# Dilated heads with the values as weights and turned outputs, and the mixture of dilations on GpSimd from SyncE's loads

## Chip, cores, metric

One core of a Trainium2 chip runs the kernel. The metric is device time in microseconds, the median of the runs. The core's engines work beside each other, each on its own queue in order: TensorE (matrix products; in the profile PE, and PEld for its weight loads), VectorE (DVE), ScalarE (ACT), GpSimd (POOL) and SyncE (SP, which here only issues DMAs; GpSimd issues some too). A matrix instruction holds one operand in the array, the weights, and streams the other through it; its result lands in PSUM, from where VectorE or ScalarE takes it to SBUF. A product of fp32 operands is two such instructions.

## What is computed

An encoder layer over two sequences, of 1024 and 256 rows (1280 in all, ten tiles of 128). Two attention branches run in parallel on the same input: eight windowed heads with a sink, and twelve dilated heads, four for each of the dilations 1, 4 and 16. Each dilated head attends within its residue class; the three dilations of one head are then mixed with a softmax over their log-sums:

```
def _dilated_mixture(q, k, v, bias_b):
    for gi, (window, dil) in enumerate(B_GROUPS):            # (128,1), (512,4), (2048,16)
        hs = slice(gi * 4, (gi + 1) * 4)
        o, lse = _banded_attention(_to_residues(q[:, :, hs], dil), _to_residues(k[:, :, hs], dil),
                                   _to_residues(v[:, :, hs], dil), window // (2 * dil), dil, bias_b[:, hs], None)
        outs.append(_from_residues(o, dil)); lses.append(_from_residues(lse, dil))
    alpha = jax.nn.softmax(jnp.stack(lses), axis=0)
    return jnp.sum(alpha[..., None] * jnp.stack(outs), axis=0)

merged = gate0 * (o_a @ w_branch_a) + gate1 * (o_b @ w_branch_b)
x = x + merged @ w_out
```

Gates, output product, a squared-ReLU MLP and two norms follow. The large products are carried out in three passes over operands split into a rounded high part and a low rest.

## The kernel before

The queue order of every engine is written out by hand, as generators whose steps are drawn at fixed places; nothing is reordered. Four stages matter here.

*Values and pairs.* The input product is made column block by column block (`pair`, products `seven`, `prompt` and `six`, L351). `tick` is called between parts of it; in the last seven of sixteen pairs every second tick draws one step of `attention_b`.

*Dilated heads*, `attention_b`. `order` has 60 tiles: two head pairs, three dilations, ten tiles of 128 queries in residue order. A tile is one piece of 128 queries against 256 or 128 keys or, at the two ends of a sequence or residue class, two pieces of 64 queries, each with its own 128 keys. A step handles two tiles. In this order it issues: the value loads; `values_of` and `store_values` for the tiles of two steps before; `transposes` for those of the step before (L553); `scores` (products L522, bias and maximum L533); `exponentials` with their sums (L543). `values_of` (L566) holds the turned probabilities `pt` (128 keys x 128 queries) as weights and streams 64 columns of v for each head, so its output has queries on the partitions and the two heads side by side. `store_values` takes one tile on ScalarE and one on VectorE into `o`, a row of 2*64 outputs, two negated maxima and two sums (`ROW`, 132 numbers), and GpSimd stores it to `scr_b` (L575), 72 stores in all.

*Windowed heads*, the loop at L1275: 40 tiles, two per iteration j, with `scores`, `exponential`, `transposes` and `values_of` (L1110) like those above, only that `values_of` here holds 64 columns of v as weights and streams 128 columns of `pt`, each head's output in its own half of the partitions. The output tile `o` (two buffers) is stored by GpSimd (L1114). Between them the loop draws from `fill`, the gate products `logits` (L192): a weight column block is fetched by SyncE (`fetch`, L222), split by ScalarE and VectorE (`prepare`, L231, L235), and results go to `scr_g` through SyncE (L1136). GpSimd loads the next unit's bias (L454).

The same loop draws twice per iteration, from j = 4 on, from `merges`: for each head pair and each two tiles `load_rows` has GpSimd load the rows of the three dilations back in natural order (L1148 to L1159, 76 loads in all), and `merge` makes on VectorE the mixture weights from the maxima and sums (L1167 to L1178), weighs the rows (L1182) and adds them (L1187, L1188) into `merged`, 128 queries to a partition block. At the loop's end, and in the next stage at places listed in `side`, `turn_merged` turns a tile with two TensorE transposes (L1216) and ScalarE makes its high part `ob_hi` (L1224); `low_b` makes the low part (L1228). The next stage is the list `jobs`, gated branch products (L192 again), which read `ob_hi` and `ob_lo` as the streamed operand.

Tiles come from tags with a fixed number of buffers: `wslot` ("w", ten of 4 KB a partition, for weights, gate results and the rows `r`), `slot` ("m", 33), PSUM banks by tag ("mm" 3, "sc" 2, "pt" 2, "pv" 1). An instruction that writes a tile waits until the buffer's earlier readers are done.

## Time and profile before

| | |
|---|---|
| time before, median of 3 runs | 1723.88 us (1721.58 to 1724.01) |
| the profiled execution | 1723.0 us, its span 1721.2 us |
| granted TensorE clock | 0.999 |
| stage of the dilated heads | about 356 to 535 us |
| stage of the windowed heads and the mixture | about 555 to 710 us |
| branch products (`jobs`) from | about 712 us |

The span runs from the first to the last instruction. A row of the order of time gives start, length, engine, line of the kernel, operation, output and inputs, shapes and how many were put together; in square brackets stands idle time before it and what ended it. For a matrix instruction `pv<-v,pt 128*128 128x64` is: into pv, weights of 128 rows by 128 columns, a streamed operand of 128 partitions by 64 columns. Its printed length contains the run through the array, which overlaps the next one's; the distance from start to start is what it costs. A row of a group gives, after the count, busy time in us, the mean ns of one, and idle time before it with what ended it.

### The profile page before, as it was taken

Reading aid. Unit: us, or ns where it says so; the run is one execution under the profiler, and the core shown is the slowest. Engines: PE = TensorE matmul, PEld = TensorE weight load, DVE = VectorE, ACT = ScalarE, POOL = GpSimd, SP = SyncE. Lnnn points to the kernel's source line nnn. Section 1 sums busy time; section 2 is a strip of 40 time slices with the busy share of each in tenths; the row PEclk is TensorE's granted clock in tenths of the full one; section 3 lists DMA queues with packets and bytes.
Section 4 is the critical chain, followed back from the end, with each engine's and each line's share of the span. In section 5 each row is a group of like instructions: output and inputs, shape, how many; then the busy total and the mean of one; then the engine's idle time right before and its main releaser. Section 6 shows DMA issues by size and latency. Waiting matters only on the chain.

```text
span 1721.2 us, 25157 instructions
## 1 busy us (share of the span) xinstructions
PE 1690.8 (98%) x9248; PEld 1430.4 (83%) x9248; DVE 973.6 (57%) x1688; ACT 727.0 (42%) x1528; POOL 516.2 (30%) x442
## 2 busy tenths in 40 slices
PE   7999999999999999999999999999999999999998
PEld 6898888888888888788888788888888888888886
DVE  6732323445553566677368545455556876667575
ACT  6232323355553555655166333333334433333344
POOL 0213222212322244300100445565555342314140
PEclk9999999999999999999999999999999999999999
DMA  6414343576666753656012334433446834633333
GB/s 239 145 43 140 115 137 95 150 196 178 173 171 176 208 174 104 221 181 230 25 74 74 122 120 157 149 115 127 157 136 232 308 130 158 209 115 117 117 116 123
DMA packets 213738, 256.34 MB, mean 149 GB/s; under 512 B 24487, under 2 KB 144123, under 8 KB 213488
## 3 DMA queue, kind: packets, MB, share of 16 engines
q1 hardware_dynamic: 200704, 228.26, 41.1%
q0 software_dynamic: 11824, 24.38, 4.6%
q10 hardware_dynamic: 1088, 2.10, 0.3%
q8 instruction: 73, 1.20, 0.3%
q14 instruction: 49, 0.40, 0.1%
HBM read 169.10 MB, written 90.73 MB: 151 GB/s over the span
## 4 chain that ended last, share of the span: by engine, by line
PE 87%; DVE 4%; ACT 2%; issue 2%; DMA 2%; POOL 1%; SPq 0%; DVEq 0%; ACTq 0%; POOLq 0%
PE dn L351 21%; PE x L351 18%; PE mm L192 12%; PE z L351 9%; PE v L739 5%; PE pv L351 5%; PE mm L351 5%; PE y L351 4%; PE pv L566 2%; PE sc L522 2%; PE pt L553 1%; PE pv L1110 1%; PE pt L1095 1%; PE tr L342 1%; DVE clo L318 1%
## 5 line engine op out<-in xcount | busy, mean ns | idle before, releaser
L351 PE MATMUL dn<-dhi,ulo 128*128 128x512 f32 x448 | 174.6, 390 | 2.9 <-DVE ulo L186 2.9
L351 PE MATMUL dn<-dlo,uhi 128*128 128x512 f32 x448 | 174.3, 389 | 0.0
L351 PE MATMUL dn<-dhi,uhi 128*128 128x512 f32 x448 | 174.3, 389 | 0.0
L351 PE MATMUL x<-chi,wlo 128*128 128x512 f32 x424 | 167.6, 395 | 2.0 <-DVE u L1760 1.4
L351 PE MATMUL x<-clo,whi 128*128 128x512 f32 x424 | 165.7, 391 | 0.1
L351 PE MATMUL x<-chi,whi 128*128 128x512 f32 x424 | 165.1, 389 | 0.0
L318 DVE TENSOR_TENSOR wlo<-ta,whi 128x1024 fp32r<-128x1024 f32 x30 | 55.7, 1857 | 180.9 <-ACT whi L316 180.9
L318 DVE TENSOR_TENSOR wlo<-raw,whi 128x1024 fp32r<-128x1024 f32 x60 | 89.4, 1491 | 102.2 <-ACT whi L316 102.2
L393 POOL TENSOR_TENSOR tb<-raw 128x512 f32<-128x512 f32 x25 | 33.6, 1345 | 340.8 <-PE mm L192 114.9
L351 PEld LDWEIGHTS dn<-dhi,ulo 128*128 128x128 f32 x448 | 84.1, 188 | 21.4 <-DVE ulo L186 3.9
L186 DVE TENSOR_TENSOR ulo<-uraw,uhi 128x1024 fp32r<-128x1024 f32 x56 | 95.2, 1720 | 11.7 <-ACT uhi L185 11.7
L351 PEld LDWEIGHTS dn<-dhi,uhi 128*128 128x128 f32 x448 | 84.1, 188 | 17.5
L351 PEld LDWEIGHTS dn<-dlo,uhi 128*128 128x128 f32 x448 | 84.1, 188 | 17.3
L351 PEld LDWEIGHTS x<-chi,wlo 128*128 128x128 f32 x424 | 79.7, 188 | 20.3 <-issue 3.1
L351 PEld LDWEIGHTS x<-chi,whi 128*128 128x128 f32 x424 | 79.6, 188 | 17.2
L351 PEld LDWEIGHTS x<-clo,whi 128*128 128x128 f32 x424 | 79.8, 188 | 14.8 <-DVE clo L318 0.4
L1585 POOL TENSOR_TENSOR t<-raw,t 128x1024 f32<-128x1024 f32 x16 | 46.0, 2897 | 143.1 <-DMA raw<-in_w_down_dram 143.1
L1736 DVE TENSOR_TENSOR v<-v,dn 128x512 f32<-128x512 f32 x90 | 59.5, 682 | 42.8 <-PE dn L351 38.7
L1832 POOL TENSOR_TENSOR u<-u,u 128x640 f32<-128x640 f32 x16 | 25.6, 1598 | 162.4 <-ACT u L1757 162.4
L351 PE MATMUL pv<-phi,wlo 128*128 128x256 f32 x256 | 72.5, 283 | 1.7 <-ACT u L1756 1.7
L351 PE MATMUL dn<-dhi,up 128*128 128x512 f32 x224 | 73.5, 389 | 0.0
L543 ACT ACTIVATE s<-s,o 128x128 f32<-128x128 f32 (+1 forms) x120 | 51.9, 434 | 50.5 <-DVE o L535 46.5
(338 smaller groups left out, 4724.2 us busy)
## 6 DMA issues: line engine op xcount, KB each, us to landing
scr_u<-u SPq DMA_DIRECT2D x112, 320.0 KB, 2.6
uraw<-scr_u SPq DMA_DIRECT2D x56, 512.0 KB, 4.2
raw<-in_w_in_dram SPq DMA_DIRECT2D x33, 512.0 KB, 6.0
raw<-in_w_up_dram SPq DMA_DIRECT2D x32, 512.0 KB, 5.4
raw<-in_w_down_dram SPq DMA_DIRECT2D x28, 512.0 KB, 6.5
sg<-scr_g SPq DMA_DIRECT2D x32, 256.0 KB, 6.2
uraw<-scr_u SPq DMA_DIRECT2D x28, 256.0 KB, 4.7
v<-scr_v SPq DMA_DIRECT2D x96, 64.0 KB, 2.4
```

What stands on the lines that cost most here:

```text
L186: nc.vector.tensor_tensor(lo, src, hi.bitcast(F32), op=ALU.subtract)
L192: nc.tensor.matmul(ps, a, b, start=i == 0, stop=i == len(seq) - 1)
L318: nc.vector.tensor_tensor(lo, src, hi.bitcast(F32), op=ALU.subtract)
L351: nc.tensor.matmul(ps, a, b, start=first and i == 0, stop=last and i == len(seq) - 1, skip_group_check=True)
L393: (nc.vector if vector else nc.gpsimd).tensor_tensor(o, x, y, op=ALU.subtract)
L522: nc.tensor.matmul(at(k, h)[p0 : p0 + nq, :], qk[rows, p0 : p0 + nq], qk[rows, P + P * a : P + P * a + W], start=True, stop=True, skip_gro ...
L543: nc.scalar.activation(s[:, h, :W], s[:, h, :W], AF.Exp, bias=nm[:, h : h + 1], accum_out=l[:, h : h + 1])
L566: nc.tensor.matmul(pv[p0 : p0 + nq, HD * h : HD * h + HD], pt[:, 2 * k + h, p0 : p0 + nq], v[:, a + k, HALVES[h]], start=k == 0, stop=k == ...
L739: nc.tensor.matmul(ps[:, :n], a, b, start=k == 0 and j == 0, stop=k == KC - 1 and j == 2)
L1585: nc.gpsimd.tensor_tensor(o, a, b, op=ALU.subtract)
L1736: nc.vector.tensor_tensor(v, v, ps, op=ALU.add)
L1832: nc.gpsimd.tensor_tensor(u[S1], u21, u22, op=ALU.add)
```

## The change

Dilated heads. `values_of` now holds 64 columns of v as weights and streams `pt`, the heads alternating innermost, into the two halves of the partitions: outputs have head and channel on the partitions and queries along the row. `store_values` takes both tiles of a step with one copy, on VectorE and ScalarE in turn, and stores runs of queries that are contiguous into `scr_b[g][i]` (128 x 1280), 54 stores in all. Maxima and sums no longer go with the rows; they stay in two const tiles `nm_b`, `l_b` (128 x 120), at columns that `places` gives.

The mixture. `merge` is one generator. Once, it turns the two tiles of statistics (two TensorE transposes), copies them with VectorE, stores them with 13 GpSimd DMAs into `scr_n`, and reads them back with 12 (`spread`: each partition gets 1/32 of every class, in pieces of 16 to 128 bytes, 4,608 in all). After four more draws VectorE puts them into natural order and computes, for all heads at once, what the old `merge` computed for two tiles; the weights go back in residue order with 6 GpSimd DMAs to `scr_c`. Then 18 items follow, one per draw: block of up to 512 queries, head pair, dilation. SyncE loads the outputs and, for each head, its weights broadcast over 64 partitions (three DMAs an item, two items ahead); GpSimd multiplies and, for dilations 4 and 16, adds, reading across the residue classes, into `merged`, which is now turned as the products need it. `turn_merged` is gone; `high_b` and `low_b` split a whole block at once.

```
-    scr_b = [dram.tile([T, 2, ROW], F32, name=f"scr_b{g}_") for g in range(3)]
+    scr_b = [[dram.tile([P, T], F32, name=f"scr_b{g}{i}") for i in range(2)] for g in range(3)]
+    scr_n = dram.tile([2, ROWS * P], F32, name="scr_n")
+    scr_c = dram.tile([1, ROWS * P], F32, name="scr_c")
...
-                o = make("o", (P, ROW), n=8)
...
-                nc.vector.tensor_scalar(o[:, 2 * HD : 2 * HD + 2], m, -1.0, None, op0=ALU.mult)
-                live[k] = s, o
+                nc.vector.tensor_scalar(nm_b[:, places(k)], m, -1.0, None, op0=ALU.mult)
+                live[k] = s
...
-        def values_of(j, whole):
+            live[j] = pt
+
+        def values_of(j, pv):
 
             _, _, _, (pieces, W, _) = order[j]
-            pt, v = live[j][0], held.pop(j)[1]
-            pv = whole[:, P * (j % 2) : P * (j % 2) + P]
-            for h in range(2):
-                for a, (p0, nq, _, _) in enumerate(pieces):
-                    for k in range(W // P):
-                        nc.tensor.matmul(pv[p0 : p0 + nq, HD * h : HD * h + HD], pt[:, 2 * k + h, p0 : p0 + nq],
-                                         v[:, a + k, HALVES[h]], start=k == 0, stop=k == W // P - 1,
+            pt, v = live.pop(j), held.pop(j)[1]
+            c = P * (j % 2)
+            for a, (p0, nq, _, _) in enumerate(pieces):
+                for k in range(W // P):
+                    for h in range(2):
+                        nc.tensor.matmul(pv[HALVES[h], c + p0 : c + p0 + nq], v[:, a + k, HALVES[h]],
+                                         pt[:, 2 * k + h, p0 : p0 + nq], start=k == 0, stop=k == W // P - 1,
                                          skip_group_check=True)
 
-        def store_values(j, eng, whole):
-            g, i, _, (pieces, _, _) = order[j]
-            o = live.pop(j)[1]
-            moved(eng, o[:, : 2 * HD], whole[:, P * (j % 2) : P * (j % 2) + P])
-            for p0, nq, qa, _ in pieces:
-                nc.gpsimd.dma_start(scr_b[g][qa : qa + nq, i, :], o[p0 : p0 + nq, :])
+        def store_values(j, eng, pv):
+            o = make("o", (P, 2 * P), n=3)
+            moved(eng, o, pv[:, : 2 * P])
+            runs = []
+            for k in (j, j + 1):
+                g, i, _, (pieces, _, _) = order[k]
+                for p0, nq, qa, _ in pieces:
+                    c = P * (k % 2) + p0
+                    if runs and runs[-1][0] + runs[-1][2] == c and runs[-1][1] + runs[-1][2] == qa:
+                        runs[-1][2] += nq
+                    else:
+                        runs.append([c, qa, nq])
+            for c, qa, nq in runs:
+                nc.gpsimd.dma_start(scr_b[g][i][:, qa : qa + nq], o[:, c : c + nq])
...
-                store_values(j - 4, nc.scalar, pv)
-                store_values(j - 3, nc.vector, pv)
+                store_values(j - 4, (nc.vector, nc.scalar)[j // 2 % 2], pv)
...
-        def load_rows(i, t):
...
-        def merge(i, t):
-
-            r = rows_b.pop((i, t))
-            nm, ls = r[:, :, :, 2 * HD : 2 * HD + 2], r[:, :, :, 2 * HD + 2 :]
...
-                nc.vector.tensor_tensor(o, o, e[:, j].unsqueeze(3).to_broadcast([P, 3, 2, HD]), op=ALU.mult)
-            yield
-            if t // 4 not in merged:
-                merged[t // 4] = slot("merged", (P, 4, 2 * P))
-            m = merged[t // 4][:, t % 4 : t % 4 + 2, P * i : P * i + P]
-            nc.vector.tensor_tensor(m, r[:, :, 0, : 2 * HD], r[:, :, 1, : 2 * HD], op=ALU.add)
-            nc.vector.tensor_tensor(m, m, r[:, :, 2, : 2 * HD], op=ALU.add)
-            yield
-
...
+        def merge():
+
+            cb = slot("cb")
+            ps = bank("mm", "tn")
+            for i, x in enumerate((nm_b, l_b)):
+                nc.tensor.transpose(ps[:ROWS, P * i : P * i + P], x, ident)
+            rows = cb[:ROWS, : 2 * P].rearrange("p (x q) -> p x q", x=2)
+            nc.vector.tensor_copy(rows, ps[:ROWS, : 2 * P].rearrange("p (x q) -> p x q", x=2))
+            a = scr_n[:, :]
+
+            def dump(r0, n, step, c0, m, base, stride):
+                dst = bass.AP(a.tensor, a.offset + base, [[stride, n], [ROWS * P, 2], [1, m]])
+                nc.gpsimd.dma_start(dst, rows[r0 : r0 + (n - 1) * step + 1 : step, :, c0 : c0 + m])
+
+            for x in range(4):
+                dump(8 * x, 7, 1, 0, P, NS * x + 64, P)
...
+            dump(72, 48, 1, 0, P, 9 * NS, P)
...
+            for g in range(3):
+                for b, sl in ((0, slice(0, 32)), (2, slice(32, 40))):
+                    R = place(g, b)[3]
+                    for x in range(2):
+                        dst = (raw[:, g, x, sl] if g else nat[:, x, 0, sl]).rearrange("p (r j) -> p r j", r=R)
+                        nc.gpsimd.dma_start(dst, spread(scr_n, g, b, x))
...
+            for _ in range(5):
+                yield
+            for g in (1, 2):
+                for b, sl in ((0, slice(0, 32)), (2, slice(32, 40))):
+                    R = place(g, b)[3]
+                    nc.vector.tensor_copy(nat[:, :, g, sl].rearrange("p x (j r) -> p x j r", r=R),
+                                          raw[:, g, :, sl].rearrange("p x (r j) -> p x j r", r=R))
...
+                    nc.gpsimd.dma_start(spread(scr_c, g, b), out[:, g, sl].rearrange("p (r j) -> p r j", r=R))
+            yield
+            yield
...
+            items = [(b, i, g) for b in range(3) for i in range(2) for g in range(3)]
+            held = {}
+
+            def load(k):
+                if k >= len(items):
+                    return
+                b, i, g = items[k]
+                t0, n = BLOCKS[b]
+                base, length, stride, R = place(g, b)
+                r = held[k] = wslot("r", (P, 2, n))
+                q0, nq = t0 % NS // R, n // R
+                src = scr_b[g][i][:, NS:] if b == 2 else scr_b[g][i][:, :NS]
+                src = src.rearrange("p (r q) -> p r q", r=R)[:, :, q0 : q0 + nq]
+                nc.sync.dma_start(r[:, 0, :].rearrange("p (r q) -> p r q", r=R), src)
+                a = scr_c[:, :]
+                for h in range(2):
+                    nc.sync.dma_start(
+                        r[HALVES[h], 1, :].rearrange("p (r q) -> p r q", r=R),
+                        bass.AP(a.tensor, a.offset + base + (2 * i + h) * length + q0, [[0, HD], [stride, R], [1, nq]]))
+
+            load(0)
+            yield
+            load(1)
+            yield
+            for k, (b, i, g) in enumerate(items):
+                load(k + 2)
+                r = held.pop(k)
+                n = BLOCKS[b][1]
+                R = place(g, b)[3]
+                if b not in merged:
+                    merged[b] = slot("merged", (P, 2, n))
+                m = merged[b][:, i, :]
+                nc.gpsimd.tensor_tensor(r[:, 0, :] if g else m, r[:, 0, :], r[:, 1, :], op=ALU.mult)
+                if g:
+                    m = m.rearrange("p (q r) -> p q r", r=R)
+                    nc.gpsimd.tensor_tensor(m, m, r[:, 0, :].rearrange("p (r q) -> p q r", r=R), op=ALU.add)
+                yield
...
-        def turn_merged(t, tag="pt"):
...
-            for j in range(2):
-                nc.tensor.transpose(ps[:, P * j : P * j + P], merged[t // 4][:, t % 4, P * j : P * j + P], ident)
...
+        def high_b(b):
+
+            ob_hi.block(b)
+            ob_lo.block(b)
+            nc.scalar.activation(ob_hi.t[b, 0], merged[b], AF.Copy)
+
+        def low_b(b):
+            nc.vector.tensor_tensor(ob_lo.t[b, 0], merged[b], ob_hi.t[b, 0].bitcast(F32), op=ALU.subtract)
...
-        merges = merges_of([(i, t) for t in range(0, NT, 2) for i in range(2)])
+        merges = merge()
...
-                if j >= n - 4:
-                    turn_merged(j - n + 4, "mm")
...
-            if j >= n - 4 and j < n:
-                low_b(j - n + 4)
-                turn_merged(j - n + 5, "mm")
-                low_b(j - n + 5)
+            if j == n - 4:
+                high_b(0)
...
-        side = {0: [(turn_a, 0)], 1: [(low_a, 0), (turn_a, 1)], 2: [(low_a, 1), (turn_merged, 4)],
-                3: [(low_b, 4), (turn_a, 2), (widen, 4)], 4: [(low_a, 2), (turn_a, 3)], 5: [(low_a, 3), (turn_merged, 5)],
-                6: [(low_b, 5), (turn_merged, 6)], 7: [(low_b, 6), (turn_merged, 7)], 8: [(low_b, 7)],
+        side = {0: [(turn_a, 0)], 1: [(low_a, 0), (turn_a, 1)], 2: [(low_a, 1)],
+                3: [(turn_a, 2), (widen, 4)], 4: [(low_a, 2), (turn_a, 3)], 5: [(low_a, 3)],
+                6: [(high_b, 1)], 7: [(low_b, 1)],
                 9: [(turn_a, 4), (widen, 6)], 10: [(low_a, 4), (turn_a, 5)], 11: [(low_a, 5)],
                 13: [(turn_a, 6), (widen, 8)], 14: [(low_a, 6)], 15: [(turn_a, 7)], 16: [(low_a, 7)],
-                17: [(turn_merged, 8)], 18: [(low_b, 8), (turn_merged, 9)], 19: [(low_b, 9)],
+                17: [(high_b, 2)], 18: [(low_b, 2)],
                 20: [(turn_a, 8)], 21: [(low_a, 8)], 22: [(turn_a, 9)], 23: [(low_a, 9)]}
```

`place(g, b)` and `spread` only compute addresses: base, class length, stride and number of classes of dilation g in block b (1 class for dilation 1; 4 and 8 in the longer sequence, 2 and 2 in the shorter). In the branch stage `run(merges)` stands behind `sums_a()` instead of ahead of it.

113 lines of the change are left out of this document (55 added, 58 removed).

## The prediction

> **What bounds the kernel now.** The page comes first, then the busy time by stretch of time, then the order of time on TensorE.
>
> ```profile
> span 1721.2 us, 25157 instructions
> PE 1690.8 (98%) x9248; PEld 1430.4 (83%) x9248; DVE 973.6 (57%) x1688; ACT 727.0 (42%) x1528; POOL 516.2 (30%) x442
> PE 87%; DVE 4%; ACT 2%; issue 2%; DMA 2%; POOL 1%; SPq 0%; DVEq 0%; ACTq 0%; POOLq 0%
> ```
>
> ```profile
> 356.00:535.00 179.00, 179.00 (x1318) 149.20 (x1317) 96.62 (x400) 100.32 (x336) 44.79 (x80) 1.00 0.62 176
> 575.00:600.00 25.00, 24.00 (x181) 19.41 (x180) 16.51 (x68) 12.94 (x36) 11.96 (x20) 1.00 0.55 152
> ```
>
> The second fence has, for each stretch, its length, then busy time of TensorE, its weight loads, VectorE, ScalarE and GpSimd, the granted clock (1.00) and the DMA share. The dilated heads run in 356 to 535: TensorE has no idle time in it, VectorE and ScalarE are a little over half busy. The windowed heads, with the mixture of dilations beside them, start at about 555: TensorE is idle for about 1 us in 25. So what counts is first how long the matrix instructions take, then whether anything new keeps TensorE waiting. The chain of waits agrees: 87% of it is TensorE.
>
> **The value products of the dilated heads.** A step handles two tiles. There are 30 steps of three kinds: 6 with two tiles of 256 keys (kind A), 12 with one of these and one of two pieces (B), 12 with two tiles of 128 keys (C). One step of each, in order of time (start, length, engine, instruction, count):
>
> ```profile
> 512.23 1.89 PE L566 MATMUL pv<-v,pt 128*128 128x64 f32 x16
> 513.96 0.50 PE L553 MATMUL pt<-ident,s 128*128 128x128 f32 x3
> ...
> 445.01 0.39 PE L351 MATMUL y<-hhi,whi 128*128 128x512 f32 x1
> 445.24 1.38 PE L566 MATMUL pv<-v,pt 128*128 128x64 f32 x16
> 446.55 0.66 PE L553 MATMUL pt<-ident,s 128*128 128x128 f32 x4
> 447.14 0.72 PE L522 MATMUL sc<-qk 64*128 64x128 f32 x8
> ...
> 370.01 1.00 PE L566 MATMUL pv<-v,pt 128*128 128x64 f32 x8
> 370.85 0.61 PE L553 MATMUL pt<-ident,s 128*128 128x128 f32 x4
> 371.39 0.71 PE L522 MATMUL sc<-qk 64*128 64x128 f32 x8
> ```
>
> From start to next start: A 1.73 us for 16 instructions, B 1.31, C 0.84 for 8. In A and C the weights are 128x128 and one instruction costs 0.11 us although it streams only 64 columns. In B, by the code, eight instructions are of that sort (0.84, from C), so the eight of the two-piece tile, with 64-column weights whose outputs lie in alternate partition halves, cost 0.47 together.
>
> The change makes all of them of this latter sort: weights are 64 columns of v, 128 query columns stream, the heads alternate between output halves, innermost. The windowed heads do exactly that already (L1110):
>
> ```profile
> 588.52 0.40 PE L192 MATMUL mm<-hhi,whi 128*128 128x512 f32 x1
> 588.85 1.53 PE L1110 MATMUL pv<-pt,va 128*64 128x128 f32 x24
> 590.31 0.50 PE L192 MATMUL mm<-hhi,wlo 128*128 128x512 f32 x1
> ...
> 601.53 0.39 PE L192 MATMUL mm<-hhi,whi 128*128 128x512 f32 x1
> 601.85 1.09 PE L1110 MATMUL pv<-pt,vp 128*64 128x128 f32 x16
> 602.87 0.38 PE L192 MATMUL mm<-phi,wlo 128*128 128x256 f32 x1
> ```
>
> 24 take 1.46 us, 16 take 1.02: 0.055 each and 0.14 fixed. Entering costs: 601.53 to 601.85 is 0.32, where 512-column instructions otherwise stand 0.23 apart, so 0.09. Leaving costs: the four transposes take 0.59 behind B (446.55 to 447.14), 0.54 behind C, so 0.05. New prices: A 1.02 + 0.14 = 1.16; C 0.58 + 0.14 = 0.72; B 0.58 for its wide eight, 0.22 for the narrow eight at half the columns, 0.09 to enter (leaving is paid today) = 0.89. Were the narrow eight no cheaper than wide ones (0.44), B would be 1.11. Saved: 6 x 0.57 + 12 x 0.42 + 12 x 0.12 = **9.9 us**; with the bound for B 7.3. As TensorE has no idle time there, all of it shortens the stage.
>
> The rest of that step costs nothing on the path: one evacuation of 256 columns in place of two of 128 (VectorE 96.62 of 179 busy), the maxima and sums into const tiles instead of beside the outputs, 54 stores instead of 72 from GpSimd (44.79 of 179). Cover gone, an evacuation would hold the single pv bank, but the next value products come some 5 us later.
>
> **The turns removed.** Ten turn_merged, two transposes each, leave TensorE.
>
> ```profile
> 717.15 0.39 PE L192 MATMUL mm<-obhi,whi 128*128 128x512 f32 x1
> 717.38 0.38 PE L1216 MATMUL tm<-ident,merged 128*128 128x128 f32 x2
> 717.51 0.48 PE L192 MATMUL mm<-obhi,wlo 128*128 128x512 f32 x1
> 717.82 0.40 PE L192 MATMUL mm<-oblo,whi 128*128 128x512 f32 x1
> ...
> PEld tm L1216 <- DVE o L1254: 0.6, 1, 0.6
> ```
>
> 717.15 to 717.82 is 0.67 for two instructions that take 0.46 without a turn: 0.21 each, 2.1 in all. One turn waits 0.6 besides (last row, from the list of waits: total, times, longest). Saved: **2.7**. The splits move to ScalarE and VectorE in three wide pieces of the same bytes. Two new transposes at the start of the stage: **+0.3**.
>
> **The mixture.** VectorE loses the ten merges; GpSimd loses 76 loads and gets 13 stores of the statistics, 12 loads that spread them, 6 stores of weights, then 18 items (dilation, head pair, block), each a multiplication and, for two dilations in three, an addition. SyncE's queue gets 54 loads.
>
> ```profile
> L1182 DVE TENSOR_TENSOR r<-r,e 128x384 f32<-128x384 f32 x20 | 10.2, 550 | 0.0
> L1153 POOL DMA_DIRECT2D r<-scr_b__83 x16 | 9.6, 603 | 1.3 <-DMA scr_o<-o 1.3
> L454 POOL DMA_DIRECT2D bias<-wide x4 | 3.0, 752 | 14.2 <-issue 10.1 <-DMA r<-scr_b__82 2.5 <-DMA r<-scr_b__81 1.6
> L393 POOL TENSOR_TENSOR tb<-raw 128x512 f32<-128x512 f32 x25 | 33.6, 1345 | 340.8 <-PE mm L192 114.9 <-DMA raw<-in_w_up_dram 92.6 <-DMA raw<-in_w_in_dram 72.0
> L393 POOL TENSOR_TENSOR tb<-raw,ta 128x512 f32<-128x512 f32 x25 | 43.0, 1720 | 2.0
> L1114 POOL DMA_DIRECT2D scr_o<-o x20 | 11.4, 571 | 84.0 <-DVE mm__5752 L1168 16.0 <-DVE o L1113 13.5 <-DVE mm__7224 L1168 7.3
> ...
> L318 DVE TENSOR_TENSOR wlo<-ta,whi 128x1024 fp32r<-128x1024 f32 x30 | 55.7, 1857 | 180.9 <-ACT whi L316 180.9
> L318 DVE TENSOR_TENSOR wlo<-tb,whi 128x1024 fp32r<-128x1024 f32 x30 | 36.5, 1217 | 11.7 <-ACT whi L316 11.7
> ...
> 552.23 0.67 POOL L1148 DMA_DIRECT2D r<-scr_b__81  x1 [7.81 <-PE x L351]
> 575.46 0.59 POOL L1114 DMA_DIRECT2D scr_o<-o  x1 [15.97 <-DVE mm__5752 L1168]
> ...
> r<-scr_b__81 POOLq DMA_DIRECT2D x20, 66.0 KB, 4.5
> scr_o<-o POOLq DMA_DIRECT2D x20, 128.0 KB, 2.2
> raw<-in_w_in_dram SPq DMA_DIRECT2D x33, 512.0 KB, 6.0
> ```
>
> Spreading, in today's times: GpSimd begins where its loads begin now, 552. Thirteen stores at 0.60 are 8, landing some 3, then 12 loads of together 4,608 pieces of 16 to 128 bytes. No row shows such pieces. Lower bound 0.60 a load, 7 us; upper bound by L454, 256 pieces in 0.75, or 2.9 ns a piece: 13.5. I take 10. With 4.5 to land (last rows: KB each, us from issue to landing) they are there at 575 to 581. The weight arithmetic on VectorE, which would block everything behind it, comes four steps of the generator later, behind the value products of j = 8, at 590: 9 us to spare. Were it not enough, score reductions and evacuations would stand behind the waiting copies, and TensorE behind them. The output store of 575.46 is delayed by at most a few us, and its tile has a second buffer (6.5 us, below). SyncE's first weight load waits for the 6 stores of weights, some 6 us in which gate stores and weight fetches queue behind it; a fetch lands well before it is split:
>
> ```profile
> 592.50 0.38 SPq L222 DMA_DIRECT2D raw<-in_w_in_dram  x1
> ...
> 611.88 1.04 ACT L231 ACTIVATE whi<-raw 128x1024 fp32r<-128x1024 f32 x1
> ```
>
> 19 us from issue to use, of which such a load needs 6 (the row of DMA issues above). So 0.
>
> Items: two iterations stand 13.0 us apart (588.85 and 601.85), two generator steps in each: 3.25 us an item. A multiplication costs 1.35 to 1.72. The addition reads with steps of 256 or 512 bytes and more, which no row shows; bounds 1.35 and, at three times the contended row, 5.2. I take 2.3, nearer the plain rows, since count and width are theirs. A mean item is then 1.5 + 2/3 x 2.3 = 3.0, under 3.25, and half that in the last block. GpSimd just keeps up: 0.
>
> What I do charge: beside GpSimd's arithmetic VectorE's subtraction L318 takes 1857 ns, where it takes 1217 with GpSimd quieter. Two weight splits of this stage fall beside the items, 0.64 each; transposes wait behind them: **+1.0**. [...]
>
> VectorE's relief (550 ns twice per merge, and eight smaller operations) may shorten other waits; I count 0, at best 2.
>
> **Sum.** -9.9 - 2.7 + 0.3 + 1.0 = -11.3. The profiled execution took 1723.0 us, 0.9 below the median of the three runs and within their 1721.58 to 1724.01. 1723.0 - 11.3 = **1711.7**. Own range: best 1723.0 - 12.3 - 2 = 1708.7, worst with B's bound 1714.3 and 2 us of small waits, 1716; a run scatters by about 1.5.
>
> **Rivals.**
> 1. *GpSimd's queue becomes the pace* (slower side). If the strided addition costs 6.5 us, an item is 5.8: over the 12 items of the first two blocks the lag grows by 12 x 2.55 + 6 x 0.6 for output stores = 34 us. The output stores stand in the same queue; their two buffers cover 13 us less 2.2 for landing, some 11; then VectorE waits for a buffer and TensorE behind it: +23. Time 1723.0 - 12.3 + 23 = 1733.7. It costs from a mean item of about 3.9 us, (11 - 3.6) / 12 + 3.25, and turns the gain into a loss at about 4.9. For it: GpSimd is busy for 11.96 of 25 us with loads already. Against: these loads go. [...]
> 2. *The statistics arrive late.* At 6 ns a piece, twice L454's, loading takes 28 us; they land at 595 (552 + 8 + 3 + 28 + 4.5), 5 us after VectorE wants them, and the weight stores and SyncE are late in turn: 5 + 1 us. Time 1717.7. For it: 16-byte pieces are unlike any row. Against: 9 us of slack.
> 3. *The two heads do not overlap* (the change does not do what it says). Then each wide instruction costs 0.11: A 1.76 + 0.28 = 2.04, C 1.16, B 1.55, or 6 x 0.31 + 12 x 0.32 + 12 x 0.24 = 8.6 lost in place of 9.9 won: 1723.0 + 8.6 - 2.7 + 0.3 + 1.0 = 1730.2. Against: the loop order is that of L1110.
>
> **How the numbers follow.** Forecast 0.62, rival 1 0.15 (a third of it only within 0.2%), rival 2 0.14, rival 3 0.04, something else about even 0.05. A measurement of this kernel can tell 0.2%, 3.4 us, from no change. Faster 0.76, within 0.2% 0.09, slower 0.15. The range is 1707.5 (1708.7 less scatter) to 1722: the forecast's cases, all of rival 2 and the mild part of rival 1.
>
> **What would show it.** Right: L566's rows as 128*64 with 128 columns; the dilated stage some 10 us shorter with TensorE still full; no L1216 row. Wrong: VectorE idle before the copies of the statistics (rival 2); idle before the output copy L1113, released by a DMA behind a late GpSimd store, and addition rows on GpSimd over 4 us (rival 1); value products 0.11 us apart (rival 3). SyncE held by free w buffers, so that the fetch L222 lands after its split is due, would prove me wrong where I charged 0.

## The result and the profile after

The changed kernel takes 1709.72 us (median of 4 runs, 1707.90 to 1711.55) against 1723.74 us (4 runs, 1721.58 to 1724.01) for the kernel before on the same chip: ratio 0.9921, 95% interval 0.9904 to 0.9939. The forecast was 1711.7. The profiled execution took 1707.9 us.

The page of the changed kernel, its span, busy times and shares of the chain of waits:

```profile
span 1706.1 us, 24925 instructions
PE 1678.4 (98%) x9230; PEld 1411.9 (83%) x9230; DVE 953.8 (56%) x1553; ACT 718.6 (42%) x1485; POOL 511.0 (30%) x409
PE 90%; DVE 4%; ACT 2%; issue 1%; POOL 1%; DMA 1%; SPq 0%; ACTq 0%; DVEq 0%; POOLq 0%
```

Its busy time by stretch (length, then TensorE, weight loads, VectorE, ScalarE, GpSimd, granted clock, DMA share): the dilated heads, 25 us of the windowed heads, and that whole stage:

```profile
358.00:523.00 165.00, 165.00 (x1279) 125.64 (x1279) 92.31 (x381) 95.35 (x319) 33.30 (x59) 1.00 0.64 185
565.70:590.70 25.00, 25.00 (x205) 21.11 (x204) 14.34 (x64) 14.01 (x41) 11.27 (x18) 1.00 0.60 156
...
552.00:690.00 138.00, 137.46 (x1091) 117.98 (x1090) 76.84 (x265) 81.01 (x221) 69.00 (x83) 1.00 0.66 191
```

The windowed stage of the kernel before, in the same view:

```profile
560.00:703.00 143.00, 140.61 (x1098) 118.48 (x1098) 91.82 (x366) 83.22 (x237) 55.81 (x89) 1.00 0.56 165
```

TensorE stays full in the dilated heads. In the windowed stage it was idle for 2.4 us and is now for 0.5, VectorE lost 15 us of work and GpSimd got 13. One step of each kind in the order of time of the changed kernel (A, B, C, as in the prediction):

```profile
500.38 1.09 PE L581 MATMUL pv<-pt,v 128*64 128x128 f32 x16
501.40 1.09 PE L568 MATMUL pt<-ident,s 128*128 128x128 f32 x8
...
437.26 0.89 PE L581 MATMUL pv<-pt,v 128*64 128x128 f32 x16
438.08 0.87 PE L568 MATMUL pt<-ident,s 128*128 128x128 f32 x6
...
371.43 0.66 PE L581 MATMUL pv<-pt,v 128*64 128x128 f32 x8
372.01 0.66 PE L568 MATMUL pt<-ident,s 128*128 128x128 f32 x4
```

From start to start A costs 1.02, B 0.82, C 0.58.

To see where the time went, each execution is cut at instructions that all kernels have, by their start in TensorE's order of time (first product into y of the pairs; first and last dilated value product; first and last windowed value product; first and last branch product; last output product; first and last down product, L355). Lengths in us, with the changed kernel run a second time (the first experiment):

| stretch | before | changed | changed again |
|---|---|---|---|
| start to first pair | 121.52 | 122.89 | 121.42 |
| first to last dilated value product | 165.99 | 156.69 | 156.69 |
| first to last windowed value product | 129.78 | 124.58 | 125.08 |
| first to last branch product | 90.39 | 86.99 | 87.43 |
| last output product to first down product | 406.38 | 408.86 | 408.92 |
| first to last down product | 383.72 | 383.68 | 385.60 |

The stretches that are not listed changed by 1 us or less each. The start and the down products differ between two executions of one kernel by 1.5 to 2 us (for the down products the last section shows why); the other rows repeat within 0.5. So the gain is 9.3 in the dilated heads, about 5.0 in the windowed stage and about 3.2 in the branch products, and 2.5 us are lost ahead of the down products, where the change touches nothing.

### The profile page after: what moved, and what is told of

Same layout as the page of the kernel before. It is cut to its first block, busy times and chain, and to the rows that moved or that the text cites. A ratio compares the mean times of both kernels' runs of the same rounds, so it can differ in the third digit from the quotient of the medians.

```text
span 1706.1 us, 24925 instructions
## 1 busy us (share of the span) xinstructions
PE 1678.4 (98%) x9230; PEld 1411.9 (83%) x9230; DVE 953.8 (56%) x1553; ACT 718.6 (42%) x1485; POOL 511.0 (30%) x409
## 4 chain that ended last, share of the span: by engine, by line
PE 90%; DVE 4%; ACT 2%; issue 1%; POOL 1%; DMA 1%; SPq 0%; ACTq 0%; DVEq 0%; POOLq 0%
PE dn L355 21%; PE x L355 19%; PE mm L192 13%; PE z L355 9%; PE v L761 6%; PE pv L355 5%; PE mm L355 5%; PE y L355 5%; PE sc L538 2%; PE pv L581 1%; PE pt L568 1%; PE pv L1132 1%; PE pt L1117 1%; PE tr L346 1%; DVE ulo L186 1%
## 5 line engine op out<-in xcount | busy, mean ns | idle before, releaser
L355 PE MATMUL dn<-dhi,ulo 128*128 128x512 f32 x448 | 175.3, 391 | 4.0 <-DVE ulo L186 4.0
L355 PE MATMUL dn<-dlo,uhi 128*128 128x512 f32 x448 | 174.9, 390 | 0.0
L355 PE MATMUL dn<-dhi,uhi 128*128 128x512 f32 x448 | 174.9, 390 | 0.0
L355 PE MATMUL x<-chi,wlo 128*128 128x512 f32 x424 | 167.7, 395 | 2.0 <-DVE u L1822 1.4
L355 PE MATMUL x<-clo,whi 128*128 128x512 f32 x424 | 165.9, 391 | 0.1
L355 PE MATMUL x<-chi,whi 128*128 128x512 f32 x424 | 165.2, 390 | 0.0
L355 PEld LDWEIGHTS dn<-dhi,ulo 128*128 128x128 f32 x448 | 84.4, 188 | 22.9 <-DVE ulo L186 5.3
L355 PEld LDWEIGHTS dn<-dhi,uhi 128*128 128x128 f32 x448 | 84.4, 188 | 17.4
L355 PEld LDWEIGHTS dn<-dlo,uhi 128*128 128x128 f32 x448 | 84.4, 188 | 17.3
L355 PEld LDWEIGHTS x<-chi,wlo 128*128 128x128 f32 x424 | 79.8, 188 | 20.3 <-issue 3.1
L355 PEld LDWEIGHTS x<-chi,whi 128*128 128x128 f32 x424 | 79.7, 188 | 17.1
L355 PEld LDWEIGHTS x<-clo,whi 128*128 128x128 f32 x424 | 79.8, 188 | 14.7 <-DVE clo L322 0.4
L558 ACT ACTIVATE s<-s,nm_b 128x128 f32<-128x128 f32 (+1 forms) x120 | 51.9, 434 | 54.6 <-DVE nm_b L550 54.6
L355 PE MATMUL pv<-phi,wlo 128*128 128x256 f32 x256 | 72.6, 283 | 1.7 <-ACT u L1818 1.7
L355 PE MATMUL dn<-dhi,up 128*128 128x512 f32 x224 | 73.5, 389 | 0.0
```

What stands on the lines that cost most here:

```text
L355: nc.tensor.matmul(ps, a, b, start=first and i == 0, stop=last and i == len(seq) - 1, skip_group_check=True)
L558: nc.scalar.activation(s[:, h, :W], s[:, h, :W], AF.Exp, bias=nm[:, h : h + 1], accum_out=l[:, h : h + 1])
```

## Experiments

Each ratio is against the kernel before, with its 95% interval; "stage" is the stretch of the table.

**The changed kernel again.**

> The changed kernel once more, as the base for the others and to see what of a stage's difference is scatter of a single execution. Expected: 1709.7 us within 1.5, dilated stage (first to last value product) 156.7 us within 0.5. If the 1.4 us lost ahead of the dilated stage and the 2.5 us lost ahead of the first down product in the profiled execution of after belong to the change, they stand here again; if they are scatter, they don't.

1709.72 us, ratio 0.9922 (0.9906 to 0.9939). The table shows it: the 1.4 us at the start are scatter, the 2.5 us ahead of the down products are not. The mean of the two executions, 124.8 and 87.2 us, is the base for the windowed stage and the branch products below.

**The old value products.**

```
-            for a, (p0, nq, _, _) in enumerate(pieces):
-                for k in range(W // P):
-                    for h in range(2):
-                        nc.tensor.matmul(pv[HALVES[h], c + p0 : c + p0 + nq], v[:, a + k, HALVES[h]],
-                                         pt[:, 2 * k + h, p0 : p0 + nq], start=k == 0, stop=k == W // P - 1,
...
+            for h in range(2):
+                for a, (p0, nq, _, _) in enumerate(pieces):
+                    for k in range(W // P):
+                        nc.tensor.matmul(pv[p0 : p0 + nq, c + HD * h : c + HD * h + HD],
+                                         pt[:, 2 * k + h, p0 : p0 + nq], v[:, a + k, HALVES[h]],
+                                         start=k == 0, stop=k == W // P - 1, skip_group_check=True)
```

> The changed kernel with the dilated value products in the form of before (probabilities as weights, 64 columns of values streamed, heads outermost); the outputs are then stored unturned, so the mixture adds what does not belong together. Theory: the 9.3 us that the dilated stage gained are the price of these products alone; the stage grows by 9 to 10 us and the time with it, to about 1719.2. Rival: a part of the gain came from the halved evacuations, the fewer stores or the maxima and sums no longer written beside the outputs; then the stage grows by clearly less, 5 to 8 us.

1717.62 us, 0.9973 (0.9962 to 0.9984). The dilated stage takes 165.99 us, to 0.01 that of the kernel before. The 9.3 us are the products' price and nothing else; the halved evacuations and the fewer stores are worth nothing there, as the prediction had it.

**The heads apart.**

```
-            for a, (p0, nq, _, _) in enumerate(pieces):
-                for k in range(W // P):
-                    for h in range(2):
+            for h in range(2):
+                for a, (p0, nq, _, _) in enumerate(pieces):
+                    for k in range(W // P):
```

> The changed kernel with the heads outermost instead of innermost in the dilated value products: the same instructions, the same operands and outputs, another order. Theory: an instruction costs 0.055 us only because its neighbour writes the other half of the partitions; with the heads apart most cost 0.11, and the dilated stage grows by 13 to 18 us (rival 3 of the prediction: 18.5 for all of them). Rival: the price comes from the weights being 64 columns wide, whatever the order; then the stage grows by 0 to 1 us.

1710.44 us, 0.9928 (0.9913 to 0.9943); the stage grew by 0.75 us. The theory falls: the products need not alternate to be cheap. The value products of the dilated stage as groups, different shapes apart (count, busy time, mean ns of one), first the kernel before, then the changed one, then this run:

```profile
L566 PE MATMUL pv<-v,pt 128*128 128x64 f32 x288 | 35.3, 269 | 0.0
L566 PE MATMUL pv<-v,pt 128*64 128x64 f32 x96 | 5.4, 234 | 0.0
```

```profile
L581 PE MATMUL pv<-pt,v 128*64 128x128 f32 x288 | 22.4, 283 | 0.0
L581 PE MATMUL pv<-pt,v 128*64 128x64 f32 x96 | 4.8, 221 | 0.0
```

```profile
L581 PE MATMUL pv<-pt,v 128*64 128x128 f32 x288 | 22.7, 284 | 0.0
L581 PE MATMUL pv<-pt,v 128*64 128x64 f32 x96 | 5.4, 227 | 0.0
```

What tells the dear group from the cheap ones is the weights' shape, 128*128 against 128*64: 64 columns behind 128-column weights cost 0.11 us, 128 columns behind 64-column weights 0.055 (A less C, 0.44 for 8). The busy time of the narrow group can't be divided by its 96 products, because each run of eight contains the end of its last one; from start to start eight of them cost B less C, 0.24, so 0.030 each. Behind 64-column weights the streamed width counts too. And an overlap is there in either order: a stretch of 0.03 us at the start of a step already holds two products, in the changed kernel (437.25 to 437.275) and in this run (437.58 to 437.61), and the two together take hardly longer than the 0.32 us of the longest single one:

```profile
437.26 0.33 PE L581 MATMUL pv<-pt,v 128*64 128x128 f32 x2
```

```profile
437.59 0.34 PE L581 MATMUL pv<-pt,v 128*64 128x128 f32 x2
```

Whether the price comes from this overlap or from the shorter load of the weights (mean of the PEld rows of these products: 191 ns for 128*128 in the kernel before, 136 ns for 128*64 in the changed one) was not separated. The heads apart cost 0.6 us of busy time in the 96 narrow products and 0.3 in the wide ones.

**Before, without the mixture's arithmetic:** 120 operations of VectorE and ten of ScalarE.

```
-            nm, ls = r[:, :, :, 2 * HD : 2 * HD + 2], r[:, :, :, 2 * HD + 2 :]
...
-            nc.vector.tensor_tensor(m, m, r[:, :, 2, : 2 * HD], op=ALU.add)
+                nc.gpsimd.memset(merged[t // 4], 0.5)
```

> The kernel before without the arithmetic of its mixture on VectorE and ScalarE (the loads of the rows, the turns and the splits stay; the merged tiles hold a constant). Theory: about 4.5 us of TensorE's stalls in the windowed stage and 1 to 2 in the jobs come from that arithmetic standing in VectorE's and ScalarE's queues, so the time falls by 4 to 6.5 us, to about 1718.5. Rival: the stalls come from late transfers (weight fetches beside the row loads) or from the turns; then it falls by 0 to 1 us.

1721.99 us, 0.9994 (0.9984 to 1.0003). The time says the rival, the stages say the theory: the windowed stage fell by 3.7 us, to 126.05. What TensorE's weight loads waited for in that stage (total, times, longest), before and then this run:

```profile
PEld pt L1095 <- DVE pt L273: 1.9, 4, 0.7
PEld pt L1095 <- ACT pt L271: 1.8, 2, 0.9
PEld sc L1071 <- DVE m L1073: 1.8, 8, 0.3
```

```profile
PEld pt L1095 <- DVE pt L273: 0.7, 1, 0.7
PEld sc L1071 <- DVE m L1073: 0.5, 2, 0.3
PEld pt L1095 <- ACT pt L271: 0.4, 1, 0.4
```

5.5 us became 1.6. In the branch products this run has a wait of its own: TensorE stands still for 3.1 us at 724.8, its weight loads waiting for a weight split of ScalarE, so that stretch grew to 91.82. Neither kernel has it, and why it arises wasn't settled; with it the time hides what the stage shows.

**Before, without the exponential of the mixture weights.**

```
-            nc.scalar.activation(e, e, AF.Exp)
```

> The kernel before without the exponential of its mixture weights on ScalarE (differences stand in for the weights); all of VectorE's mixture work stays. The run without any mixture arithmetic took 3.7 us off the windowed stage (first to last value product there, 129.8 us). Theory S: ScalarE standing in order behind VectorE's differences (5.4 us in 6 waits) holds back the copies of the turned probabilities; then this run takes 2 us or more of the 3.7. Theory V: VectorE's own mixture instructions stand ahead of its copies and score reductions; then it takes 0 to 1 us.

1724.00 us, 1.0006 (0.9996 to 1.0016); windowed stage 128.99, 0.8 less. Theory V: of the 3.7 us some 3 are VectorE's own instructions ahead of its copies and reductions, 0.8 ScalarE standing behind them.

**The items on VectorE.**

```
-                nc.gpsimd.tensor_tensor(r[:, 0, :] if g else m, r[:, 0, :], r[:, 1, :], op=ALU.mult)
+                nc.vector.tensor_tensor(r[:, 0, :] if g else m, r[:, 0, :], r[:, 1, :], op=ALU.mult)
...
-                    nc.gpsimd.tensor_tensor(m, m, r[:, 0, :].rearrange("p (r q) -> p q r", r=R), op=ALU.add)
+                    nc.vector.tensor_tensor(m, m, r[:, 0, :].rearrange("p (r q) -> p q r", r=R), op=ALU.add)
```

> The changed kernel with the 18 items' multiplications and additions on VectorE instead of GpSimd, at the same places. Theory: what the windowed stage gained beyond the turns came from VectorE's queue being rid of the mixture; 20 operations of some 0.65 us come back into that stage and wait in order for SyncE's loads, so the stage grows by 2 to 6 us and the time to 1712 to 1716. Rival: the gain came from the weights being worked out once and from ScalarE; then the stage grows by 0 to 1 us, and without GpSimd's contention nm_a falls back from 386 to about 160 ns.

1712.08 us, 0.9941 (0.9925 to 0.9958); windowed stage 127.24, 2.4 us more than the base. This run's waits of TensorE:

```profile
PEld pt L1117 <- DVE pt L275: 2.0, 2, 1.1
...
PEld sc L1093 <- DVE m L1095: 0.9, 4, 0.3
```

The old waits are back. So 2.4 of the 3.7 us hang on GpSimd doing the items (with VectorE here also standing 2.0 us for an item's load); what is left may lie in the weights being worked out once, which wasn't tried alone.

**GpSimd's items slower.** Two runs: everything twice, and the multiplications alone twice.

```
-                nc.gpsimd.tensor_tensor(r[:, 0, :] if g else m, r[:, 0, :], r[:, 1, :], op=ALU.mult)
+                for _ in range(2):
+                    nc.gpsimd.tensor_tensor(r[:, 0, :] if g else m, r[:, 0, :], r[:, 1, :], op=ALU.mult)
...
-                    nc.gpsimd.tensor_tensor(m, m, r[:, 0, :].rearrange("p (r q) -> p q r", r=R), op=ALU.add)
+                    for _ in range(2):
+                        nc.gpsimd.tensor_tensor(m, m, r[:, 0, :].rearrange("p (r q) -> p q r", r=R), op=ALU.add)
```

> The changed kernel with each of GpSimd's multiplications and additions of the mixture carried out twice (the result is weighed twice and summed too often). A mean item then takes 4.9 us (twice 1.40 + 2/3 x 1.55) against 3.25 us per draw. Theory, rival 1 of the prediction with this price: GpSimd falls behind by 12 x 1.6 + 3.6 = 23 us, the two output buffers cover 11, and the time grows by some 12 us, to about 1722. Rival: the lag stays in GpSimd's queue until the split of the first block, and the time grows by 0 to 3 us.

1726.71 us, 1.0026 (1.0015 to 1.0038): slower than before; windowed stage 143.31, 18.5 us more.

> The changed kernel with GpSimd's multiplications of the mixture carried out twice, the additions once (the outputs are weighed twice). A mean item takes 2 x 1.40 + 2/3 x 1.55 = 3.8 us. By the prediction's rival 1, where the two output buffers cover the lag, it costs from 3.9 us on: 0 to 1 us. By the run with both operations twice (4.9 us an item, 17 us lost, the splits and gate copies waiting for buffers that GpSimd's items hold), and 12 items that each add their excess, it costs from 3.45 on: 4 us or more.

1718.10 us, 0.9970 (0.9960 to 0.9980); windowed stage 132.82, 8.0 us more. What VectorE waited for with everything twice, then ScalarE, and behind it TensorE's weight loads:

```profile
DVE wlo L235 <- POOL merged L1273: 12.3, 1, 12.3
```

```profile
ACT gs L1157 <- POOL merged L1277: 9.3, 2, 6.0
...
ACT whi L231 <- POOL merged L1277: 6.7, 1, 6.7
...
PEld pt L1117 <- ACT pt L273: 13.7, 2, 8.8
```

and VectorE with the multiplications twice:

```profile
DVE wlo L235 <- POOL merged L1273: 7.8, 1, 7.8
```

Not the output buffers: the items' tiles `r` come from the ten "w" buffers that the raw weights, `whi`, `wlo` and the gate copies `gs` use too, in turn. An item that GpSimd hasn't finished holds the buffer that the next weight split or gate copy writes; ScalarE and VectorE wait there, ScalarE's copies of turned probabilities stand behind that in its queue, and TensorE waits for those (13.7 us with everything twice, 4.4 with the multiplications twice). Part of both losses is TensorE's granted clock, which is half for some 13 and some 7 us in and behind these waits.

**No items.**

```
-                nc.gpsimd.tensor_tensor(r[:, 0, :] if g else m, r[:, 0, :], r[:, 1, :], op=ALU.mult)
...
+                    nc.gpsimd.memset(merged[b], 0.5)
```

> The changed kernel without GpSimd's arithmetic of the mixture (the merged tiles hold a constant; SyncE's loads stay). The prediction's charge of 1.0 us for VectorE slowed beside GpSimd: if it is real, windowed stage and jobs shrink by about 1 us. By the rows of the changed kernel, where the weight splits keep 1225 ns and only the small nm_a grew from 162 to 386 ns: 0 to 0.5 us, with nm_a back at about 160.

1707.65 us, 0.9915 (0.9901 to 0.9930). Windowed stage 124.07 and branch products 87.80: together 0.2 us less than the base, so in the trace nothing; the medians differ by 2.1 with overlapping intervals, and 1.9 us of that stand in the down products of the profiled execution (383.70 us against 385.60 in the second of the changed kernel; the last section has the reason). VectorE's groups in the windowed stage, changed kernel, and then this run:

```profile
L235 DVE TENSOR_TENSOR wlo<-raw,whi 128x1024 fp32r<-128x1024 f32 x6 | 7.4, 1226 | 8.6 <-ACT whi L231 7.3 <-DMA scr_g<-gs 1.3
...
L1099 DVE SCALAR_TENSOR_TENSOR nm_a<-m,nsink 128x2 f32<-128x2 f32 x40 | 15.5, 386 | 1.4
```

```profile
L1099 DVE SCALAR_TENSOR_TENSOR nm_a<-m,nsink 128x2 f32<-128x2 f32 x40 | 6.5, 163 | 1.4
```

**The turns back,** called at the ten old places.

```
+        def turn_again(tag="pt"):
+            ps = bank(tag, "tm")
+            for j in range(2):
+                nc.tensor.transpose(ps[:, P * j : P * j + P], merged[0][:, j, :P], ident)
```

> The changed kernel with the ten turns of two transposes back on TensorE, at the old places, of a finished block and taken up by nobody. The prediction has 20 x 0.21 / 2 = 2.1 us for them and 0.6 for one wait. Theory: the windowed stage with its end (four turns) grows by 0.8, the jobs (six turns) by 1.3, together 2.1. Rival: a turn's 0.21 was partly time that TensorE would have spent waiting anyway, then together 1 us or less; the rest of what the jobs gained (3.4 us, 1.3 of it by the turns) is waits of the old kernel in either case.

Windowed stage 125.59, 0.8 more than the base; branch products 88.61, 1.4 more: 2.2, as the theory has it. The time, 1709.55 us (0.9921, 0.9907 to 0.9936), can't show 2 us against its scatter.

**The statistics used earlier.**

```
-            for _ in range(5):
+            for _ in range(3):
                 yield
```

> The changed kernel with the weight arithmetic drawn two draws, 6.5 us, earlier (three empty draws instead of five). The prediction counted 9 us between the landing of the statistics and their use; then nothing changes, 0 to 0.3 us. By the trace of the changed kernel the last of the loads is issued at 577.2 and lands some 2.9 us later, 2 to 3 us ahead of VectorE's copies at 582.3; then VectorE waits for some 4 us in order and the windowed stage grows by 1 to 4 us.

1719.57 us, 0.9982 (0.9973 to 0.9992): three quarters of the gain are gone; windowed stage 133.98, 9.2 us more. VectorE's copies of the statistics in the order of time, this run:

```profile
574.53 0.21 DVE L1210 COPY cb<-cb 128x64 f32<-128x64 f32 x1
575.46 0.17 DVE L1210 COPY cb<-cb 128x16 f32<-128x16 f32 x1 [0.72 <-DMA cb<-scr_n]
577.61 0.21 DVE L1210 COPY cb<-cb 128x64 f32<-128x64 f32 x1 [1.98 <-DMA cb<-scr_n]
578.92 0.17 DVE L1210 COPY cb<-cb 128x16 f32<-128x16 f32 x1 [1.09 <-DMA cb<-scr_n]
```

and GpSimd's part in the changed kernel, with VectorE's first use of what it loads:

```profile
553.81 4.66 POOL L1187 DMA_DIRECT2D scr_n<-cb  x8 [17.21 <-DVE cb L1182]
...
571.07 6.11 POOL L1204 DMA_DIRECT2D cb<-scr_n  x8 [4.53 <-issue]
```

```profile
582.34 0.49 DVE L1210 COPY cb<-cb 128x64 f32<-128x64 f32 x4
```

The last statistics land at 578.9; the changed kernel uses them at 582.3. The slack is 3.4 us, not 9. VectorE stands 3.8 us in those gaps. TensorE's weight loads wait 6.7 us for copies of turned probabilities in the stage, where the changed kernel's wait 0.5: 2.4 at 577.8, behind the statistics, and most of the rest at 641 to 645, where VectorE stands for 5.3 us before a weight split whose buffer an item holds. Behind each of these two waits the granted clock is half for some 3.4 us, at most 1.7 us more each. The items, drawn 6.5 us earlier, fall differently among the weight fetches; why just so wasn't followed.

**The lost 2.5 us.** In the order of time at the first down product, changed kernel (GpSimd, VectorE, TensorE):

```profile
1310.91 5.79 POOL L1647 TENSOR_TENSOR t<-raw 128x1024 f32<-128x1024 f32 x2 [3.89 <-DMA raw<-in_w_down_dram]
1311.09 6.69 DVE L186 TENSOR_TENSOR ulo<-uraw,uhi 128x1024 fp32r<-128x1024 f32 x2
...
1314.52 0.80 PE L355 MATMUL dn<-dhi,ulo 128*128 128x512 f32 x1 [2.89 <-DVE ulo L186]
```

and before:

```profile
1327.35 4.54 DVE L186 TENSOR_TENSOR ulo<-uraw,uhi 128x1024 fp32r<-128x1024 f32 x2
1327.94 6.20 POOL L1585 TENSOR_TENSOR t<-raw 128x1024 f32<-128x1024 f32 x2 [4.65 <-DMA raw<-in_w_down_dram]
1328.62 0.19 PEld L351 LDWEIGHTS dn<-dhi,ulo 128*128 128x128 f32 x1 [0.69 <-DVE ulo L186]
```

Both engines take two operands from SBUF, and only the order of their starts differs: before, VectorE began 0.6 us ahead and its first split was done within 1.3 us; now GpSimd begins 0.2 us ahead, and VectorE's first split ends 3.4 us after its start. The experiment takes GpSimd's two subtractions away from there:

```
             self.right(*JOBS[0], slot)
-            self.combine(*JOBS[1])
             yield
...
             self.left(*JOBS[0], 2)
+            self.combine(*JOBS[1], nc.vector)
```

> The changed kernel with the two subtractions that GpSimd makes for the second job of the last product (L1647, at 1310.9 in the trace) on VectorE instead, behind the last split of the first job. Theory: VectorE's split ulo of the first job (two of 1.2 us) took 6.69 us there because GpSimd had begun its subtraction 0.2 us ahead of it and VectorE came through only when that ended; with GpSimd quiet the two take 2.5 us, TensorE waits 1 us or less instead of 3.2 and 0.4, its clock does not fall, and the kernel is 3 to 5 us faster than the changed one, at 1705 to 1707. Rival: the split is late because its input is; then TensorE still waits 2.5 us or more there, and the time is 1709.7 within 1.

1704.46 us, 0.9893 (0.9878 to 0.9907): the fastest of all, 5.3 us below the changed kernel's median. In the order of time of this run:

```profile
1310.27 2.35 DVE L186 TENSOR_TENSOR ulo<-uraw,uhi 128x1024 fp32r<-128x1024 f32 x2
1311.55 0.19 PEld L355 LDWEIGHTS dn<-dhi,ulo 128*128 128x128 f32 x1 [0.88 <-DVE ulo L186]
```

The two stretches around the first down product take 788.4 us instead of 792.5 in the changed kernel's first execution, 4.1 less (before: 790.1); the rest is within the scatter of the start. The theory holds: the order of the two engines is what cost the time. It doesn't say why GpSimd's input comes first in the changed kernel.

## Why the prediction came out near

**Value products: 9.9 forecast, 9.3 measured.** With the prediction's 0.14 to enter and leave, A is 1.02 + 0.14 = 1.16 and C 0.72, as forecast. In B leaving is indeed paid before the change too (the first two transposes behind it start 0.16 us apart in both kernels), so it is 0.82 + 0.09 = 0.91 instead of 0.89, and the narrow eight are 0.24 where 0.22 was forecast. These prices give 9.7; the 0.4 that are left are spread over the neighbouring products and weren't followed. The reason behind the prices was only partly right: they were read as an overlap of alternating output halves, and rival 3 rested on that. The alternating order hardly matters (0.75 us of the stage with the heads apart); 64-column weights do (0.055 us a product against 0.11), and here products behind them overlapped in either order. The forecast copied a row of the same shape (L1110), which is why an untested reason didn't hurt it.

**Turns: 2.7 forecast.** 2.2 for the transposes, measured by putting them back, and the wait of 0.6 in the branch products is gone.

**Two new transposes: +0.3 forecast.** Between the last dilated and the first windowed value product, where they stand, the changed kernel takes 0.2 us more (42.46 against 42.26).

**VectorE's relief: "0, at best 2" forecast.** This is the term that was mis-sized. It is worth 3.7 us in the windowed stage, and there 3.7 and the turns' 0.8 make 4.5 of the 5.0. In the branch products 3.2 less 1.4 for the turns leaves 1.8; TensorE's weight loads waited there for 2.1 us before (the turn's 0.6 among them) and don't wait now, which fits, but no run separates it. The trace of before had the rows: 5.5 us of TensorE's waits for VectorE's and ScalarE's work in that stage. The prediction saw TensorE idle for about 1 us in 25 and didn't ask who it waited for.

**The charge of 1.0 for slowed weight splits.** It didn't appear: the splits stay at 1226 ns. What grew is nm_a, a small operation with two SBUF inputs, from 162 to 386 ns, and without the items it is at 163 again; that costs TensorE nothing that the trace shows. The reductions (128x384), with one input in PSUM, stay at 553 ns in both kernels. No run of before showed them beside GpSimd's arithmetic; that the charge of 1.0 left them out was the author's estimate, and there it was right.

**GpSimd just keeps up: 0.** The additions that read across residue classes cost 1.55 us, where the forecast took 2.3 between 1.35 and 5.2:

```profile
L1275 POOL TENSOR_TENSOR merged<-merged,r 128x512 f32<-128x512 f32 x8 | 12.4, 1552 | 0.7
L1272 POOL TENSOR_TENSOR r<-r 128x512 f32<-128x512 f32 x8 | 10.8, 1345 | 1.8 <-DMA r<-scr_c 1.1 <-ACT pt L273 0.7
```

A mean item is 2.4 us, not 3.0; the addition is 15% above the multiplication. Rival 1's threshold was wrong: it named the output buffers and 3.9 us; at 3.83 us 8.0 us are already lost, through the "w" buffers, and the line through both runs, (18.5 - 8.0) / (4.86 - 3.83) = 10.2 us per us, reaches nothing at about 3.05: a weak estimate, a straight line through two runs that both also lost to the half clock. The prediction's last sentence had these buffers, at SyncE's fetches; it was VectorE's and ScalarE's writes that waited.

**The statistics' 9 us of slack.** 3.4 in truth. The step that failed is "GpSimd begins where its loads begin now, 552": the old loads fetched rows long finished, while the new stores need the maxima and sums turned by TensorE and copied by VectorE. The last sums are made by 518.5, but the two transposes stand in TensorE's queue behind the rest of the input product, at 552.7, so the stores began at 553.8. That is 561.4 in the times of before (the first windowed value product starts at 565.8 now and at 573.4 then), 9 us later than forecast. Rival 2 was nearer than its 0.14 said; two draws earlier it happens, and costs 9.2 us.

**Not foreseen: 2.5 us ahead of the down products**, a stage that the change doesn't touch, where two engines met in another order. That everything there came some 14 us earlier is not the reason: with the items twice the first down product starts at 1334.1, later than before (1328.6), and the stretch ahead of it takes 409.1 us all the same. All ten executions built on the changed kernel, without the last experiment's edit, take 408.6 to 409.2 there, and the three built on the kernel before 406.4 to 407.4. What in the changed kernel turns the order was not found.

The sum of forecast terms was -11.3. Measured: -9.3 in the dilated stage, -5.0, -3.2, +0.2, +2.5, and -1.2 in the small stretches, -16.0; in the mean of the two executions scatter at the start and in the down products gives 1.6 of it back (spans 1721.2 to 1706.9), and the medians differ by 14.0. An underrated relief, the charge of 1.0 that didn't come and an unforeseen loss stood partly against each other: that the time came within 2 us of the forecast is in part luck.

## What to carry to other kernels

Where TensorE is nearly full, ask of each remaining idle microsecond which queue it waited for: here VectorE's queue freed of the mixture was worth 3.7 us in one stage, the turns taken from TensorE 2.2. A product that streamed 64 columns cost twice as much here behind 128-column weights (0.11 us) as one that streamed 128 columns behind 64-column weights (0.055), so try the narrow operand as the weights. Before moving work to GpSimd, list which buffers its operands share with the critical engines, and after any change of a schedule look at places where GpSimd and VectorE both read two operands from SBUF: in the two shown below the one that began second took longer, 3.38 us instead of 1.22 (VectorE) and 2.08 instead of 1.35 (GpSimd).

## What was not expected of the hardware

VectorE and GpSimd don't slow each other evenly there; the times read as if the one that begins second waited for the other. With GpSimd's subtraction of 2.48 us begun 0.2 us ahead, VectorE's first split, 1.22 us in the kernel before, ended 3.38 us after its start, 1.08 us behind the subtraction:

```profile
1310.91 2.48 POOL L1647 TENSOR_TENSOR t<-raw 128x1024 f32<-128x1024 f32 x1 [3.89 <-DMA raw<-in_w_down_dram]
```

```profile
1311.09 3.38 DVE L186 TENSOR_TENSOR ulo<-uraw,uhi 128x1024 fp32r<-128x1024 f32 x1
```

In the windowed stage the reverse occurs: GpSimd's multiplication begun 0.3 us behind a weight split takes 2.08 us, where those into r take 1.35 in the mean, while the split keeps its 1.23:

```profile
601.83 1.23 DVE L235 TENSOR_TENSOR wlo<-raw,whi 128x1024 fp32r<-128x1024 f32 x1 [1.05 <-ACT whi L231]
602.12 2.08 POOL L1272 TENSOR_TENSOR merged<-r 128x512 f32<-128x512 f32 x1 [0.49 <-PE pt L1117]
```

That one waits is a reading of these two places; what makes it wait is not shown by any run.

Behind the wait at the first down product TensorE's granted clock (the number after GpSimd's count) is half for some 3 us in the changed kernel. In the run with the heads apart TensorE stands there as long and the clock stays full:

```profile
1314.50:1317.60 3.10, 2.93 (x6) 1.83 (x6) 3.10 (x1) 0.87 (x1) 3.10 (x2) 0.50 0.05 18
```

```profile
1312.80:1315.50 2.70, 0.00 (x1) 0.01 (x1) 2.70 (x2) 2.59 (x6) 2.70 (x2) 1.00 1.03 373
1315.50:1317.60 2.10, 1.67 (x6) 1.04 (x6) 2.10 (x1) 0.00 (x0) 2.10 (x1) 1.00 0.07 25
```

So a wait of this length may or may not be followed by a half clock; what decides was not found. What the half clock costs depends on the next wait. With none of it (heads apart, no items) or with some 3.4 us of it (the changed kernel, the turns back) the stretch of the down products takes 383.7 us, since TensorE at full clock only waits longer for VectorE's second split, 1.65 us in the run with the heads apart. Where the half clock lasts some 6.8 us, as in the changed kernel run again, the stretch takes 385.0 to 385.7. That is the difference of 1.9 us between the two executions in the table.
